# Eight unused numbers per partition behind the small tiles of a two-layer diffusion step in float32

## The chip, the cores and the metric

The kernel runs on one core of one Trainium2 chip. The metric is the time of one execution on the device in microseconds (us), the median of several runs; lower is better. Profiles come from one execution recorded by the hardware profiler.

## What is computed

The reference is one inference step of a backbone with two layers, all in float32. Each layer is run for 128 context tokens and for 512 latent tokens, model width 1024:

```python
h = x * (1 + sc_a) + sh_a
qa, ka, va, ub, vb, qc, kc, vc, gcf, gcb, pd = project(h, w_in)
...
mix = jnp.concatenate([y_a, y_b, y_c, y_d], axis=-1) @ w_out
x = layer_norm(alpha * x + g_a * mix, ln_w[0], ln_b[0])
h = x * (1 + sc_f) + sh_f
x = layer_norm(alpha * x + g_f * conv_ffn(h, ffn_up, ffn_conv_w, ffn_conv_b, ffn_down), ln_w[1], ln_b[1])
```

`y_a` to `y_d` are four mixers (windowed attention, spatial gating, retention in two directions, pooling); `conv_ffn` multiplies by `ffn_up` (1024 x 5632), applies a convolution of width 3 over the tokens, gates, and multiplies by `ffn_down` (2816 x 1024). `sh`, `sc` and `g` come from `silu(c) @ w_ada`.

## The kernel before

**Tiling.** The 640 tokens (128 context, 512 latent) are columns of one activation tile: `y8` holds 8 blocks of 128 features x 640 tokens. To keep float32 accuracy with TensorE's `float32r` operands, every operand is split into a high part and a rest: `hh` and `hl` for activations, `wh` and `wl` for weights. Every product is three matmuls: `wh` with `hh`, `wl` with `hh`, `wh` with `hl`.

**Weights.** A weight stage is fetched by the SP queue into a staging tile `st` (2048 numbers per partition, two buffers; `Cols`, `Vals` and `Rows`, DMA at L162 and in `Rows.dma`). `split` (L267 to L277) makes a pair `wh`, `wl` of 1024 numbers each: ScalarE copies `st` to `wh` (L275), VectorE subtracts (L276). The pairs live in a pool of 12 buffers, which also takes `wa`, the weights of the modulation (`AdaPair`), and some of `wf`, its first columns. `Stream` hands out the pairs in a fixed order and fetches the next stage when buffers come free.

**Products.** `fm` (L601 to L603, with the first ones at L1399 to L1402): weights are the stationary operand, activations move, 384 columns for the first part of the tokens (`GA`) and 256 for the rest (`GB`). `tm` (L883 to L885): activations are stationary, weights move, 256 columns. `wo` (L1497 to L1499, `w_out`) and `dn` (L1588 to L1590, `ffn_down`): activations are stationary, weights move, 512 columns. `sc` (L822, L823) are attention scores: queries `qs` stationary, keys `kh`, `kl` moving. `hT` (L570) transposes a tile `xr` by a matmul with the identity. `ada` (L216, L263) are the modulation products.

**Memory.** There are six pools in on-chip memory, one behind the other in this order: `one` (small tiles, and `hh`, `hl`, `y8`), `par` (parameters), `stg` (the two `st`), `wp` (the twelve weight buffers), `up` (25 unit tiles of 664 numbers, for everything else that is large) and `sm` (small numbers). Every tile takes a whole multiple of 32 bytes per partition. In `one` the tiles are, in bytes: `ident` 512, `bd` 512, `epsb` 32, `mhalf` 32, `hh`, `hl`, `y8` 20480 each, `cs` 64, `lgb` 64, `lgp` 32, `s0` 2048, `row` 2048, `scT` 1024, two folds of 32, `sb0` 128, `bf` 64. `ident` begins at byte 16512, a multiple of 64; so do `hh`, `hl` and `y8` (17600, 38080, 58560). The pool ends at 84576, 32 bytes past a multiple of 64. `par` is a multiple of 64 long, so `st` (88800 and 96992) and all twelve weight buffers (105184 and every 4096 after it) begin 32 bytes past a multiple of 64. A unit tile is 2656 bytes, 41.5 times 64, so unit tiles begin alternately on a multiple of 64 and 32 bytes past one. Addresses are those of the program; the trace has none.

**Order.** The program's order is written out by hand on every engine; no planner moves an instruction.

Of the kernel before, what the change touches and what calls it, by code (L numbers as in the profile page):

```python
# [8 lines left out]
F32 = mybir.dt.float32  # L9
# [5 lines left out]
P = 128  # L15
# [15 lines left out]
NT = 5  # L31
SPLIT_COL = 384
UW = 664

C_ID, C_BD, C_MASK, C_RELF, C_TRIF, C_RELB, C_TRIB = 0, 128, 256, 896, 1024, 1152, 1280
C_IQ, C_KC, C_COS, C_SIN, C_PF = 1408, 1664, 1666, 2178, 2690
# [53 lines left out]
def kernel(  # L90
# [6 lines left out]
    V, S, G, T = nc.vector, nc.scalar, nc.gpsimd, nc.tensor  # L97
# [3 lines left out]
    one = ctx.enter_context(tc.tile_pool(name="one", bufs=1))  # L101
# [10 lines left out]
    def nm(p):  # L112
        cnt[0] += 1
        return f"{p}{cnt[0]}"

    def unit(shape, name="u"):
        u = up.tile([P, UW], F32, tag="u", name=nm(name))[:, 0:math.prod(shape[1:])]
        if len(shape) == 3:
            u = u.rearrange("p (a b) -> p a b", b=shape[2])
        elif len(shape) == 4:  # L120
            u = u.rearrange("p (a b c) -> p a b c", b=shape[2], c=shape[3])
        return u
# [21 lines left out]
    folds = [one.tile([P, 4], F32, name="fold4"), one.tile([P, 2], F32, name="fold2")]  # L144
    sb0 = one.tile([P, 2, KD, 2], F32, name="sb0")
    bf = one.tile([P, 2, KD], F32, name="bf")
    hhf = hh.bitcast(F32)

    V.memset(scT, 0.0)
    V.memset(epsb, EPS)  # L150
    V.memset(mhalf, -0.5)


# [1534 lines left out]
```

## Time and profile before

| | |
|---|---|
| median of 3 runs | 1563.03 us (1561.6 to 1563.06) |
| the profiled execution, its own time | 1563.34 us |
| span of the profiled execution | 1561.6 us |
| TensorE busy with matmuls | 1529.7 us, 98% of the span |
| VectorE busy | 959.5 us, 61% |
| ScalarE busy | 609.9 us, 39% |
| GpSimd busy | 379.7 us, 24% |
| moved by DMA | 193.22 MB, 124 GB/s on average |

The span reaches from the first to the last instruction of the profile; the execution's own time has 1.7 us around it. Busy times of TensorE are modelled at their ends, so how fast it goes is better read from the distance between the starts of consecutive matmuls.

### The profile page before, as it was taken

Reading aid. Unit: us, or ns where it says so; the run is one execution under the profiler, and the core shown is the slowest. Engines: PE = TensorE matmul, PEld = TensorE weight load, DVE = VectorE, ACT = ScalarE, POOL = GpSimd, SP = SyncE. Lnnn points to the kernel's source line nnn. Section 1 sums busy time; section 2 is a strip of 40 time slices with the busy share of each in tenths; the row PEclk is TensorE's granted clock in tenths of the full one; section 3 lists DMA queues with packets and bytes.
Section 4 is the critical chain, followed back from the end, with each engine's and each line's share of the span. In section 5 each row is a group of like instructions: output and inputs, shape, how many; then the busy total and the mean of one; then the engine's idle time right before and its main releaser. Section 6 shows DMA issues by size and latency. Waiting matters only on the chain.

```text
span 1561.6 us, 24577 instructions
## 1 busy us (share of the span) xinstructions
PE 1529.7 (98%) x9734; PEld 1358.4 (87%) x9734; DVE 959.5 (61%) x1891; ACT 609.9 (39%) x993; POOL 379.7 (24%) x458
## 2 busy tenths in 40 slices
PE   8999999999999999999999999899999999999997
PEld 5988878899999999988789988688999999998885
DVE  4775346786556655745577665567866666674456
ACT  2544462344333333533346443524433333343331
POOL 0302266054101101200013033823531101020104
PEclk9999999999999999999999999999999999999999
DMA  9644415245343443333216355161332221224311
GB/s 326 211 152 129 136 55 202 73 130 189 120 151 116 155 137 134 109 117 124 72 38 220 123 163 175 62 202 55 126 104 82 81 81 56 81 93 130 132 38 67
DMA packets 123343, 193.22 MB, mean 124 GB/s; under 512 B 11884, under 2 KB 80566, under 8 KB 123229
## 3 DMA queue, kind: packets, MB, share of 16 engines
q1 hardware_dynamic: 114701, 166.64, 32.1%
q0 software_dynamic: 8528, 25.03, 5.0%
q8 instruction: 76, 1.25, 0.3%
q14 instruction: 38, 0.31, 0.1%
HBM read 177.97 MB, written 13.66 MB: 123 GB/s over the span
## 4 chain that ended last, share of the span: by engine, by line
PE 86%; DVE 4%; POOL 4%; ACT 2%; DMA 2%; issue 1%; SPq 0%; POOLq 0%; ACTq 0%; DVEq 0%
PE fm L601 17%; PE fm L603 16%; PE fm L602 16%; PE dn L1590 6%; PE dn L1588 6%; PE dn L1589 6%; PE ada L263 2%; PE wo L1497 2%; PE wo L1498 2%; PE wo L1499 2%; POOL on L1071 1%; DVE wl L276 1%; PE po L873 1%; PE PT L858 1%; DMA st<-in_w_in_dram 1%
## 5 line engine op out<-in xcount | busy, mean ns | idle before, releaser
L601 PE MATMUL fm<-hh,wh 128*128 128x256 f32 (+1 forms) x1888 | 589.8, 312 | 0.0
L603 PE MATMUL fm<-hl,wh 128*128 128x256 f32 (+1 forms) x1888 | 583.1, 309 | 0.9 <-DVE hl L586 0.9
L602 PE MATMUL fm<-hh,wl 128*128 128x256 f32 (+1 forms) x1888 | 582.9, 309 | 0.0
L276 DVE TENSOR_TENSOR wl<-st,wh 128x1024 fp32r<-128x1024 f32 x188 | 282.7, 1512 | 164.9 <-ACT wh L275 161.8
L601 PEld LDWEIGHTS fm<-hh,wh 128*128 128x128 f32 x1888 | 356.7, 189 | 28.1 <-ACT cv L1328 11.7
L603 PEld LDWEIGHTS fm<-hl,wh 128*128 128x128 f32 x1888 | 356.6, 189 | 1.8 <-DVE hl L586 1.1
L602 PEld LDWEIGHTS fm<-hh,wl 128*128 128x128 f32 x1888 | 356.8, 189 | 0.1
L275 ACT ACTIVATE wh<-st 128x1024 fp32r<-128x1024 f32 x188 | 196.1, 1053 | 207.2 <-PE dn L1589 141.8
L1318 DVE SCALAR_TENSOR_TENSOR cv<-fm,cwT,cv 128x127 f32<-128x127 f32 x352 | 122.0, 408 | 108.3 <-ACT cv L1315 108.2
L1590 PE MATMUL dn<-wh,hl 128*128 128x512 f32 x440 | 174.0, 395 | 0.3 <-DVE hl L1524 0.2
L1588 PE MATMUL dn<-wh,hh 128*128 128x512 f32 x440 | 174.1, 396 | 0.0
L1589 PE MATMUL dn<-wl,hh 128*128 128x512 f32 x440 | 173.8, 395 | 0.0
L1315 ACT ACTIVATE cv<-fm,cwT 128x384 f32<-128x384 f32 x88 | 58.8, 673 | 203.3 <-PE fm L603 187.8
L1537 POOL TENSOR_TENSOR act<-cv,cv 128x640 f32<-128x640 f32 x28 | 45.9, 1641 | 300.3 <-DVE cv L1333 247.3
L1328 ACT ACTIVATE cv<-fm,cwT 128x255 f32<-128x255 f32 x88 | 49.6, 563 | 175.8 <-PE fm L603 175.8
L1590 PEld LDWEIGHTS dn<-wh,hl 128*128 128x128 f32 x440 | 82.5, 187 | 21.4 <-DVE hl L1524 1.2
L1589 PEld LDWEIGHTS dn<-wl,hh 128*128 128x128 f32 x440 | 82.5, 187 | 20.0
L1588 PEld LDWEIGHTS dn<-wh,hh 128*128 128x128 f32 x440 | 82.5, 187 | 19.6
L1329 DVE SCALAR_TENSOR_TENSOR cv<-fm,cwT,bnd 128x1 f32<-128x1 f32 x88 | 19.1, 217 | 89.0 <-ACT cv L1328 88.9
L1537 POOL TENSOR_TENSOR y<-cv,cv 128x640 f32<-128x640 f32 x16 | 26.8, 1678 | 182.3 <-DVE cv L1333 162.6
L1497 PE MATMUL wo<-wh,hh 128*128 128x512 f32 x160 | 64.1, 401 | 0.0
L1498 PE MATMUL wo<-wl,hh 128*128 128x512 f32 x160 | 63.2, 395 | 0.0
(306 smaller groups left out, 2036.1 us busy)
## 6 DMA issues: line engine op xcount, KB each, us to landing
st<-in_ffn_up_dram SPq DMA_DIRECT2D x44, 1024.0 KB
wa<-in_w_ada_dram SPq DMA_DIRECT2D x80, 512.0 KB
st<-in_ffn_down_dram SPq DMA_DIRECT2D x88, 256.0 KB
st<-in_w_in_dram SPq DMA_DIRECT2D x20, 1024.0 KB
xr<-xd POOLq DMA_DIRECT2D x30, 256.0 KB, 8.1
wf<-in_w_first_dram SPq DMA_DIRECT2D x24, 256.0 KB
st<-in_w_out_dram SPq DMA_DIRECT2D x24, 256.0 KB
xd<-xr SPq DMA_DIRECT2D x20, 256.0 KB
```

The costliest lines, as they stand in the source:

```text
L275: S.activation(out=oh, in_=view, func=AF.Copy)
L276: eng.tensor_tensor(out=ol, in0=view, in1=of, op=ALU.subtract)
L601: T.matmul(ps, wh[:, k, :], hh[:, k, lo:hi], start=(k == 0), stop=False)
L602: T.matmul(ps, wl[:, k, :], hh[:, k, lo:hi], start=False, stop=False)
L603: T.matmul(ps, wh[:, k, :], hl[:, k, lo:hi], start=False, stop=(k == KD - 1))
L1318: V.scalar_tensor_tensor(out=o[:, a + d:b - 1 + d], in0=ps[:, a + 1 - d:b - d], scalar=cwT[:, tap, f:f + 1], in1=o[:, a + d:b - 1 + d], op ...
L1497: T.matmul(ps, hh[:, k, c0:c0 + P], wh[:, k % 2, :], start=(k == 0), stop=False)
L1498: T.matmul(ps, hh[:, k, c0:c0 + P], wl[:, k % 2, :], start=False, stop=False)
L1537: G.tensor_tensor(out=dst, in0=a, in1=g, op=ALU.mult)
L1588: T.matmul(ps, hh[:, s_, c0:c0 + P], wh[:, k % 2, :], start=(k == 0), stop=False)
L1589: T.matmul(ps, hh[:, s_, c0:c0 + P], wl[:, k % 2, :], start=False, stop=False)
L1590: T.matmul(ps, hl[:, s_, c0:c0 + P], wh[:, k % 2, :], start=False, stop=(k == KF - 1))
```

## The change

One tile of 8 numbers per partition (32 bytes) is added behind the last tile of the pool `one`, and VectorE fills it with zeros once. Nothing reads it. All pools behind `one` move up by 32 bytes: `st` to 88832, the weight buffers to 105216. `hh`, `hl`, `y8` and the other tiles of `one` stay.

```diff
+PAD2 = 8
...
     bf = one.tile([P, 2, KD], F32, name="bf")
+    pad2 = one.tile([P, PAD2], F32, name="pad2")
     hhf = hh.bitcast(F32)
 
     V.memset(scT, 0.0)
     V.memset(epsb, EPS)
+    for x in (pad2,):
+        V.memset(x, 0.0)
     V.memset(mhalf, -0.5)
```

## Rows read from the trace of the kernel before

**Rows 1.** The page: busy time of the engines, and the chain that ended last.
```profile
PE 1529.7 (98%) x9734; PEld 1358.4 (87%) x9734; DVE 959.5 (61%) x1891; ACT 609.9 (39%) x993; POOL 379.7 (24%) x458
...
PE 86%; DVE 4%; POOL 4%; ACT 2%; DMA 2%; issue 1%; SPq 0%; POOLq 0%; ACTq 0%; DVEq 0%
PE fm L601 17%; PE fm L603 16%; PE fm L602 16%; PE dn L1590 6%; PE dn L1588 6%; PE dn L1589 6%; PE ada L263 2%; PE wo L1497 2%; PE wo L1498 2%; PE wo L1499 2%; POOL on L1071 1%; DVE wl L276 1%; PE po L873 1%; PE PT L858 1%; DMA st<-in_w_in_dram 1%
```
**Rows 2.** Instructions grouped by line and shape: xcount | busy us, mean ns | idle before.
```profile
L601 PE MATMUL fm<-hh,wh 128*128 128x384 f32 x928 | 316.6, 341 | 0.0
L601 PE MATMUL fm<-hh,wh 128*128 128x256 f32 x960 | 273.2, 285 | 0.0
L1588 PE MATMUL dn<-wh,hh 128*128 128x512 f32 x440 | 174.1, 396 | 0.0
L1497 PE MATMUL wo<-wh,hh 128*128 128x512 f32 x160 | 64.1, 401 | 0.0
L883 PE MATMUL tm<-wh,hh 128*128 128x256 f32 x160 | 46.4, 290 | 0.0
L1399 PE MATMUL fm<-hh,wh 128*128 128x384 f32 x32 | 11.4, 358 | 0.2 <-ACT wh L275 0.2
```
**Rows 3.** Timeline of TensorE, fm: start us, duration us, engine and line.
```profile
508.94 0.34 PE L603 MATMUL fm<-hl,wh 128*128 128x384 f32 x1
...
512.59 0.34 PE L603 MATMUL fm<-hl,wh 128*128 128x384 f32 x1
512.76 0.28 PE L601 MATMUL fm<-hh,wh 128*128 128x256 f32 x1
...
515.48 0.28 PE L603 MATMUL fm<-hl,wh 128*128 128x256 f32 x1
```
**Rows 4.** Timeline of TensorE, dn and tm.
```profile
800.67 0.40 PE L1588 MATMUL dn<-wh,hh 128*128 128x512 f32 x1
...
803.47 0.40 PE L1588 MATMUL dn<-wh,hh 128*128 128x512 f32 x1
...
871.43 0.28 PE L884 MATMUL tm<-wl,hh 128*128 128x256 f32 x1
...
873.99 0.28 PE L885 MATMUL tm<-wh,hl 128*128 128x256 f32 x1
```
**Rows 5.** Timeline of TensorE, attention scores of three query blocks.
```profile
88.03 0.28 PE L823 MATMUL sc<-kl,qs 128*128 128x256 f32 x1
88.15 0.22 PE L822 MATMUL sc<-ckh,qs 128*128 128x128 f32 x1
...
92.17 0.39 PE L822 MATMUL sc<-kh,qs 128*128 128x384 f32 x1
92.40 0.34 PE L823 MATMUL sc<-kl,qs 128*128 128x384 f32 x1
...
96.78 0.39 PE L822 MATMUL sc<-kh,qs 128*128 128x384 f32 x1
97.01 0.34 PE L823 MATMUL sc<-kl,qs 128*128 128x384 f32 x1
```
**Rows 6.** Single lines: count, duration ns min/median/max, first and last start.
```profile
L570 PEld LDWEIGHTS hT<-ident,xr x120: 137/141/144, 295.8 to 1100.0; 128*128 128x128 f32 x120
...
L1333 DVE SCALAR_TENSOR_TENSOR cv<-fm,cwT,cv x88: 482/484/485, 344.6 to 1401.2; 128x256 f32<-128x256 f32 x88
...
L276 DVE TENSOR_TENSOR wl<-st,wh x188: 1206/1225/2640, 20.6 to 1510.4; 128x1024 fp32r<-128x1024 f32 x188
...
L1309 DVE TENSOR_TENSOR hl<-y,hh x10: 1206/1208/1224, 249.6 to 1044.8; 128x1024 fp32r<-128x1024 f32 x10
...
L275 ACT ACTIVATE wh<-st x188: 1039/1052/1077, 19.5 to 1509.3; 128x1024 fp32r<-128x1024 f32 x188
...
L1308 ACT ACTIVATE hh<-y x10: 1042/1044/1059, 248.5 to 1030.1; 128x1024 fp32r<-128x1024 f32 x10
```
**Rows 7.** Line L276 in 420 to 640 us and in 700 to 800 us.
```profile
L276 DVE TENSOR_TENSOR wl<-st,wh 128x1024 fp32r<-128x1024 f32 x30 | 53.7, 1789 | 10.0 <-ACT wh L275 10.0
...
L276 DVE TENSOR_TENSOR wl<-st,wh 128x1024 fp32r<-128x1024 f32 x12 | 14.7, 1224 | 37.9 <-ACT wh L275 37.9
```
**Rows 8.** The two stretches, all engines: us, busy (x count), PEclk, DMA share, GB/s.
```profile
420.00:640.00 220.00, 220.00 (x1511) 206.01 (x1510) 129.69 (x269) 73.89 (x103) 24.54 (x19) 1.00 0.39 133
700.00:800.00 100.00, 100.00 (x440) 80.37 (x439) 53.43 (x77) 33.71 (x46) 5.30 (x11) 1.00 0.27 87
```
**Rows 9.** Timeline of the start: VectorE, then TensorE's weight loads, [idle before <- releaser].
```profile
1.07 0.06 DVE L150 MEMSET epsb<- 128x1 f32 x1
1.08 0.06 DVE L151 MEMSET mhalf<- 128x4 f32 x1
4.11 0.16 DVE L1423 TENSOR_TENSOR fold<-ident 128x4 f32<-128x4 f32 x1 [2.97 <-DMA ident<-in_consts_dram]
...
8.95 0.18 PEld L216 LDWEIGHTS ada<-wf,scT 128*32 128x32 f32 x2 [0.48 <-DMA wf<-in_w_first_dram]
9.63 0.18 PEld L216 LDWEIGHTS ada<-wf,scT 128*32 128x32 f32 x2 [0.51 <-DMA wf<-in_w_first_dram]
10.30 0.14 PEld L216 LDWEIGHTS ada<-wf,scT 128*32 128x32 f32 x2 [0.48 <-DMA wf<-in_w_first_dram]
10.96 0.14 PEld L216 LDWEIGHTS ada<-wf,scT 128*32 128x32 f32 x2 [0.52 <-DMA wf<-in_w_first_dram]
11.64 0.14 PEld L216 LDWEIGHTS ada<-wf,scT 128*32 128x32 f32 x2 [0.55 <-DMA wf<-in_w_first_dram]
```
**Rows 10.** The longest pieces of the chain: start us, us, what.
```profile
8.26 11.21 DMA st<-in_w_in_dram
...
208.35 4.61 DMA st<-in_w_out_dram
```

## The prediction

> **What bounds the kernel.** I read the page first. TensorE is busy for 98% of the span, and of the chain that ended last 86% is TensorE; VectorE, the busiest of the others, has 4% of the chain [rows 1]. So only two things can move the time much: the pace at which matmuls follow each other, or a wait for staged weights that now ends earlier or later. I therefore went to the groups by line and shape for the counts and to the timeline for the pace.
>
> The counts [rows 2] stand for one of three equal lines each: fm has 3 x (928 + 32) = 2880 matmuls of 384 columns and 3 x 960 = 2880 of 256; dn and wo have 3 x (440 + 160) = 1800 of 512; tm has 3 x 160 = 480 of 256. The pace is the distance from start to start. In fm, 21 steps from 508.94 to 512.59 us make 173.8 ns for 384 columns, and 23 steps from 512.76 to 515.48 us make 118.3 ns for 256 [rows 3]. In dn, 12 steps from 800.67 to 803.47 us make 233.3 ns for 512, and in tm 22 steps from 871.43 to 873.99 us make 116.4 ns for 256 [rows 4]. Together this is 2880 x 173.8 + 2880 x 118.3 + 1800 x 233.3 + 480 x 116.4 ns = 1317 us, 84% of the span. These are the instructions whose weight operand moves.
>
> **The change, part by part.**
>
> *The new memset.* VectorE gets one more memset of 128x8. The nearest are 128x1 and 128x4, 0.06 us each, and after them VectorE is idle for 2.97 us until a DMA lands [rows 9]. That wait covers it: 0. Without the cover it would cost 0.06 us.
>
> *Staging on VectorE and ScalarE.* The splits L275 and L276 read and write tiles that begin 32 bytes past a multiple of 64. The same work on tiles that begin on a multiple of 64 already stands in the trace: L1308 and L1309 go from `y8` to `hh` and `hl`. VectorE takes 1206/1225 ns (shortest/median) for the first and 1206/1208 for the second, ScalarE 1039/1052 against 1042/1044 [rows 6]. L1333 writes `cv`, a unit tile, of which half begin on a multiple of 64 and half off it: all 88 lie between 482 and 485 ns [rows 6]. The offset costs these engines 17 ns at most (1225 - 1208), on engines that are not the bound; 188 x 17 ns = 3.2 us of VectorE's time, and on the chain L276 has 1%, 15.6 us, of which 17/1225 is 0.2 us. I take 0, with 0.2 us as the lower end. That L276 is long on average is another matter: in a stretch where GpSimd is busy 11% it means 1789 ns, where GpSimd is busy 5%, 1224 [rows 7, 8].
>
> *Unit tiles and small tiles.* All move by 32 bytes, so those that began on a multiple of 64 leave it and the others reach it. There are 25, and L1333 shows no difference between the two kinds: 0.
>
> *DMA into the moved tiles.* The first `wf` tiles are unit tiles, and consecutive ones begin alternately on a multiple of 64 and off it. The matmuls that wait for them start at 8.95, 9.63, 10.30, 10.96 and 11.64 us: 0.68, 0.67, 0.66 and 0.68 us apart, no alternation [rows 9]. So a transfer of 256 KB does not land sooner on either: 0. The rule that would say otherwise is in the Trainium skill, DMA: Bandwidth & Descriptors, section How a descriptor splits into AXI transactions: reads start at a 256-byte boundary and bytes before the start are fetched in vain. The staging tiles go from 224 to 0 bytes past such a boundary; if it held for the destination, a packet of 1024 bytes would need 32 beats in place of 39, an estimate from the page, and an 18% shorter staging transfer would take at most 2.8 us off the two pieces of 11.21 and 4.61 us in which the chain follows one [rows 10]; the sum would be near 1560. The `wf` tile that begins on a 256-byte boundary is the one that lands at 11.64 us, and its 0.68 us is no shorter than the rest.
>
> *Matmuls.* This is the only term that could decide. `hh` and `hl` stay on a multiple of 64; the weights reach it. No row shows the weights there, so I bound it. Per column, the paces are 0.4526 ns (fm 384), 0.4621 (fm 256), 0.4557 (dn) and 0.4547 (tm). In fm the off-64 operand is stationary, in dn, wo and tm it moves, and the four lie within 2%: which operand is off hardly shows. For the gain, let all come down to the best: fm 256 by 2.4 ns to 115.9, dn and wo by 1.6 ns to 231.7, tm by 0.5 ns: 2880 x 2.4 + 1800 x 1.6 + 480 x 0.5 ns = 10.0 us. For the loss, let fm 384 go to dn's pace, 175.0 ns, and tm to that of fm 256: 2880 x 1.2 + 480 x 1.9 ns = 4.4 us. The nearest row is a score matmul of 256 columns whose `kl` and `qs` both begin on a multiple of 64: its successor starts 0.12 us later, fm's 118.3 again [rows 5]. With `qs` off 64, the `kh` of 384 columns that is on 64 is followed after 0.23 us (92.17 to 92.40) and the one that is off it after 0.23 us too (96.78 to 97.01) [rows 5]. As the stationary operand, `xr` in L570 begins on a multiple of 64 in some loads and off it in others, and 120 loads lie within 137 to 144 ns [rows 6]. I take 0, with ends of -10.0 and +4.4 us.
>
> *Sum.* 0. Against the profiled execution's own 1563.34 us that is 1563.34; the median of the runs lies 0.3 us below it, so I forecast 1563.0. About 0.2%, 3.1 us, is what a measurement of this kernel can tell from no change; the three runs span 1.5 us.
>
> **The rivals.**
>
> *Weight loads or moving weights get cheaper (faster, 0.10).* For it: fm 256 takes 1.9 ns more than tm 256, and the difference between them is which operand is off 64. If that is the cause, 2880 x 1.9 = 5.5 us go and the time is 1557.5; with all of the bound it is 1553. Against it: the score row with both operands on 64 shows no such gain [rows 5].
>
> *One operand off 64 holds back every product (faster, 0.02).* Each of the 8040 products has exactly one operand off 64 now and none after. The clock granted is full, 2.4 GHz [rows 8], at which 384, 256 and 512 columns at one per cycle are 160.0, 106.7 and 213.3 ns. If the excess came from the offset, 2880 x 13.8 + 2880 x 11.6 + 1800 x 20.0 + 480 x 9.7 ns = 114 us would go: 1449. The same score row speaks against it. The Trainium skill, TensorE: Matmul & The Clock Gate, section Back-to-back issue gap, gives N/2.4 + 2.5 ns; by that rule 8040 x 2.5 ns less would go, and the time would be 1469, an estimate from the page. The trace disagrees with that rule by some 17 ns at 512 columns.
>
> *The long splits were long because of the offset (faster, 0.03).* With 1225 ns in place of the mean the chain's 15.6 us for L276 would shrink by about a fifth, 3.1 us: 1559.9. Against it, rows 7 and 8: they are long where GpSimd works.
>
> *Both operands on the same step of 64 bytes get in each other's way (slower, 0.10).* The place is fm 384, where the moving rows are on 64 already and the loads for the next matmul would now be read in step with them. The price is the upper end, 4.4 us: 1567.4. It decides from 1.1 ns per matmul (3.1 us / 2880). For it: nothing but that two operands on 64 is new for every product. Against it: the score row again.
>
> *That the layout doesn't move* would give 1563.0 as well, and lies in the forecast.
>
> **How the numbers follow.** No change has 0.75: every operand kind has a row on both sides of 64, and none differs. Faster is 0.10 + 0.02 + 0.03 = 0.15, slower 0.10. Within 0.2% of the forecast is 1559.9 to 1566.1, which holds 0.75; the staging rival ends at its edge. Down to 1557.5 about half of the first rival comes in, so 1557.5 to 1566.1 holds a little over 0.8.
>
> **What would show it.** Right: the steps of fm stay at 173.8 and 118.3 ns, dn's at 233.3, tm's at 116.4; L276 keeps 1206 as its shortest and L275 its 1052; the new memset stands near 1.1 us with VectorE idle behind it. Wrong: a step of fm 256 at 116 ns (first rival), steps near 160, 107 and 213 (second), a mean of L276 near 1225 (third), a step of fm 384 at 175 or more (fourth). A time that moves with all these unchanged would refute the view that only pace and staging count.

## The result, and the profile after

The changed kernel takes 1542.74 us (median of 4 runs, 1540.83 to 1544.91) where the kernel before takes 1562.78 in the same job: a ratio of 0.9875, 95% interval 0.986 to 0.989. The forecast was 1563.0 and no change. The profiled execution took 1542.5 us, its span is 1540.7 us, 20.9 us shorter.

The page of the changed kernel, busy times first and then two of its costliest groups (xcount | busy us, mean ns of one | idle before), answers to [rows 1] and [rows 7]; four lines were added, so L276 is now L280:

```profile
PE 1508.5 (98%) x9734; PEld 1346.0 (87%) x9734; DVE 957.4 (62%) x1892; ACT 609.7 (40%) x993; POOL 380.3 (25%) x458
...
L280 DVE TENSOR_TENSOR wl<-st,wh 128x1024 fp32r<-128x1024 f32 x188 | 282.0, 1508 | 162.1 <-ACT wh L279 159.0
...
L279 ACT ACTIVATE wh<-st 128x1024 fp32r<-128x1024 f32 x188 | 196.0, 1053 | 200.9 <-PE dn L1593 138.0
```

TensorE has lost 21.2 us of busy time with matmuls, VectorE, ScalarE and GpSimd have kept theirs within 2.1 us, and TensorE is again busy for 98% of the span. The granted clock is not what changed: it is 1.00 from 330 to 660 us in both kernels, and 0.994 before and 0.993 after over the whole execution. So the matmuls themselves follow each other faster at the same clock. The timeline of TensorE in the changed kernel shows which (start us, duration us, engine and line); it answers to [rows 3, 4]:

```profile
473.01 0.34 PE L606 MATMUL fm<-hh,wl 128*128 128x384 f32 x1
...
476.83 0.34 PE L607 MATMUL fm<-hl,wh 128*128 128x384 f32 x1
477.00 0.28 PE L605 MATMUL fm<-hh,wh 128*128 128x256 f32 x1
...
479.61 0.28 PE L607 MATMUL fm<-hl,wh 128*128 128x256 f32 x1
...
748.72 0.39 PE L1593 MATMUL dn<-wl,hh 128*128 128x512 f32 x1
...
781.23 0.40 PE L1594 MATMUL dn<-wh,hl 128*128 128x512 f32 x1
```

From 473.01 to 476.83 us are 22 steps of fm with 384 columns: 173.6 ns, as before. From 477.00 to 479.61 are 23 steps with 256 columns: 113.5 ns in place of 118.3. From 748.72 to 781.23 are 142 steps of dn: 228.9 ns in place of 233.3. Averaged over all stretches of at least 13 equal matmuls without a gap, the steps are, in ns, before and after: fm 384 173.6 and 173.7, fm 256 118.3 and 113.8, dn 233.3 and 228.9, wo 233.3 and 229.0, tm 117.0 and 117.3. With the counts of [rows 2], 2880 x 4.4 + 1800 x 4.4 ns = 20.6 us are gone and 2880 x 0.1 + 480 x 0.3 ns = 0.4 us came back: 20.2 us of the 20.9. (These means are good to some 0.2 ns.) Added up directly, from the start of each matmul to the next start on TensorE, fm 256 takes 13.1 us less, dn and wo together 7.1 us less and fm 384 0.6 us more; the rest of the difference lies outside these products.

The start of the changed kernel, VectorE's timeline, has the new memset where it was expected, with idle time behind it:

```profile
1.08 0.07 DVE L154 MEMSET pad<- 128x8 f32 x1
1.10 0.06 DVE L155 MEMSET mhalf<- 128x4 f32 x1
4.04 0.17 DVE L1427 TENSOR_TENSOR fold<-ident 128x4 f32<-128x4 f32 x1 [2.89 <-DMA ident<-in_consts_dram]
```

### The profile page after: what moved, and what is told of

It reads as the page before. It is cut to its first block, busy times and chain, and to the rows that moved or that the text cites. A ratio compares the mean times of both kernels' runs of the same rounds, so it can differ in the third digit from the quotient of the medians.

```text
span 1540.7 us, 24578 instructions
## 1 busy us (share of the span) xinstructions
PE 1508.5 (98%) x9734; PEld 1346.0 (87%) x9734; DVE 957.4 (62%) x1892; ACT 609.7 (40%) x993; POOL 380.3 (25%) x458
## 4 chain that ended last, share of the span: by engine, by line
PE 79%; DVE 4%; POOL 4%; ACT 2%; issue 1%; POOLq 0%; ACTq 0%; DVEq 0%
PE fm L605 16%; PE fm L607 15%; PE fm L606 15%; PE dn L1594 6%; PE dn L1592 6%; PE dn L1593 6%; PE ada L267 2%; PE wo L1501 2%; PE wo L1503 2%; PE wo L1502 2%; POOL on L1075 1%; DVE wl L280 1%; PE PT L862 1%; ACT h L585 1%; POOL p L1116 1%
## 5 line engine op out<-in xcount | busy, mean ns | idle before, releaser
L280 DVE TENSOR_TENSOR wl<-st,wh 128x1024 fp32r<-128x1024 f32 x188 | 282.0, 1508 | 162.1 <-ACT wh L279 159.0
L279 ACT ACTIVATE wh<-st 128x1024 fp32r<-128x1024 f32 x188 | 196.0, 1053 | 200.9 <-PE dn L1593 138.0
L1594 PE MATMUL dn<-wh,hl 128*128 128x512 f32 x440 | 173.3, 394 | 0.5 <-DVE hl L1528 0.5
L1503 PE MATMUL wo<-wh,hl 128*128 128x512 f32 x160 | 63.0, 394 | 0.0
```

The source lines that it names most:

```text
L279: S.activation(out=oh, in_=view, func=AF.Copy)
L280: eng.tensor_tensor(out=ol, in0=view, in1=of, op=ALU.subtract)
L1503: T.matmul(ps, hl[:, k, c0:c0 + P], wh[:, k % 2, :], start=False, stop=(k == KD - 1))
L1594: T.matmul(ps, hl[:, s_, c0:c0 + P], wh[:, k % 2, :], start=False, stop=(k == KF - 1))
```

## The experiments

In what follows the *distance* is the start of a weight tile minus the start of `hh`, modulo 256 bytes. `hl` and `hh` are a multiple of 256 apart, as are the twelve buffers, and so are the offsets of all blocks within a tile, so one number describes every product of a kernel. The kernel before has 32, the changed one 64. The three questions of the first four runs were: is it the weights, is it their place modulo 64, or is it the distance?

**The weights alone.** In place of the new tile in `one`, one pool of 32 bytes stands ahead of the weight buffers and one behind them, so that staging, unit and small tiles keep their place modulo 64.

```diff
+    padw_pool = ctx.enter_context(tc.tile_pool(name="padw", bufs=1))
     wp = ctx.enter_context(tc.tile_pool(name="wp", bufs=NW))
+    padu_pool = ctx.enter_context(tc.tile_pool(name="padu", bufs=1))
     up = ctx.enter_context(tc.tile_pool(name="up", bufs=NU))
...
+    padw = padw_pool.tile([P, 8], F32, name="padw")
+    padu = padu_pool.tile([P, 8], F32, name="padu")
...
```

> Only the twelve weight buffers move by 32 bytes, onto a multiple of 64; the staging tiles stay 32 bytes off, unit tiles and small tiles keep their place modulo 64. Theory A (the pace of matmuls depends on where the weights begin): the whole gain, about 1543 us, with steps of fm 256 at 113 ns and of dn at 229 ns. Rival (staging, DMA or unit tiles carry the gain): near 1563 us, steps unchanged at 118 and 233 ns.

1547.35 us (1542.2 to 1550.54), a ratio of 0.9889 (0.9866 to 0.9913). The weights carry the gain: dn stands at 228.9 ns, and staging and unit tiles have not changed their place modulo 64; of the DMA targets only `wa` and the `wf` tiles that lie in the weight buffers have. The lowest of the four runs, 1542.2 us, reaches the changed kernel. The profiled one is the slowest, 1550.54 us, and its timeline shows something new, fm with 256 columns in the first layer and in the second:

```profile
477.41 0.28 PE L607 MATMUL fm<-hh,wh 128*128 128x256 f32 x1
...
480.02 0.28 PE L609 MATMUL fm<-hl,wh 128*128 128x256 f32 x1
...
1201.99 0.28 PE L607 MATMUL fm<-hh,wh 128*128 128x256 f32 x1
...
1204.70 0.28 PE L609 MATMUL fm<-hl,wh 128*128 128x256 f32 x1
```

23 steps make 113.5 ns in the first and 117.8 ns in the second. At this distance fm has two paces. From 1100 to 1383 us, in the second layer's `ffn_up`, every stretch of 256 columns went at the second and every one of 384 columns at 176.7 ns in place of 173.2; in the first layer's, until 640 us, nearly all went at the first. In the profile of the changed kernel both layers' `ffn_up` went at the first, but for a few stretches at its beginning and end; fm in the projections ahead of it took now one pace and now the other. Added up from start to start, fm takes 6.9 us more in this profile than in that of the changed kernel, of the 8.0 us between their spans.

**Everything by 64 bytes.** `PAD2 = 16`: the weights are off 64 again, distance 96.

> Sixteen unused numbers in place of eight: all pools behind move by 64 bytes, the weights are again 32 bytes past a multiple of 64. Theory A1 (the weights' place modulo 64 decides): back to about 1563 us, steps 118 ns (fm 256) and 233 ns (dn). Rival A2 (the distance that counts is longer than 64 bytes, or any other place than the old one will do): a time that is neither 1563 nor need be 1543, and steps that differ from 118 and 233 ns.

1562.03 us, ratio 0.9998 (0.9987 to 1.0008). A memset of the same kind, all pools moved, and no gain: the place decides, not that something was moved or added. The timeline of this run has 23 steps of 118.7 ns in fm:

```profile
472.17 0.28 PE L604 MATMUL fm<-hh,wh 128*128 128x256 f32 x1
...
474.90 0.28 PE L606 MATMUL fm<-hl,wh 128*128 128x256 f32 x1
```

**The activations moved as well, and both off 64.** In the third run the eight numbers stand ahead of `hh` and not behind the small tiles: weights on a multiple of 64, `hh` 32 past one, distance 32 as before. In the fourth they stand in both places: both operands 32 past a multiple of 64, distance 64.

```diff
+    pada = one.tile([P, 8], F32, name="pada")
     hh = one.tile([P, KD, W], F32R, name="hh")
...
```

> Eight unused numbers ahead of hh in place of behind the small tiles: weights on a multiple of 64 as in the changed kernel, but hh, hl and y8 32 bytes past one, so that the distance from activations to weights is as in the kernel before. Theory R (the distance between the two operands decides): about 1563 us, steps 118 and 233 ns. Theory A1 (the weights' own place decides): about 1543 us, steps 113 and 229 ns. If both operands need a multiple of 64: in between or slower, with fm 384, whose moving operand now is off, above 173.6 ns.

> Eight unused numbers ahead of hh and eight behind the small tiles: activations and weights both begin 32 bytes past a multiple of 64, their distance is that of the changed kernel. Theory R (distance): about 1543 us, steps 113 ns (fm 256) and 229 ns (dn). Theory A1 (own place): 1563 us or slower, with no step of fm 256 under 118 ns.

The third took 1561.13 us, ratio 0.9989 (0.9978 to 0.9999); the fourth 1544.45 us, ratio 0.9882 (0.9862 to 0.9901). So a multiple of 64 is neither enough nor needed: with the weights on one and the old distance the gain is gone, and with both operands off it and the new distance it is there. The timelines of TensorE agree. The third run, fm 256 and dn:

```profile
472.68 0.28 PE L604 MATMUL fm<-hh,wh 128*128 128x256 f32 x1
...
475.39 0.28 PE L606 MATMUL fm<-hl,wh 128*128 128x256 f32 x1
...
757.11 0.39 PE L1592 MATMUL dn<-wl,hh 128*128 128x512 f32 x1
...
790.24 0.39 PE L1593 MATMUL dn<-wh,hl 128*128 128x512 f32 x1
```

That is 117.8 ns (23 steps) and 233.3 ns (142 steps), the paces of before. The fourth run, the same two:

```profile
469.95 0.28 PE L605 MATMUL fm<-hh,wh 128*128 128x256 f32 x1
...
472.56 0.28 PE L607 MATMUL fm<-hl,wh 128*128 128x256 f32 x1
...
749.74 0.39 PE L1593 MATMUL dn<-wl,hh 128*128 128x512 f32 x1
...
782.25 0.39 PE L1594 MATMUL dn<-wh,hl 128*128 128x512 f32 x1
```

113.5 ns and 228.9 ns, the paces of after.

**Other distances.** Four more values of `PAD2`, 24, 40, 56 and 48, give distances 128, 192, 0 and 224.

> All pools behind the small tiles move by 96 bytes: weights on a multiple of 64, their distance from hh 128 past a multiple of 256 (32 before, 64 in the changed kernel). Theory R64 (any distance that is a multiple of 64 will do): about 1543 us, steps near 113 ns (fm 256) and 229 ns (dn). Rival R128 (the place within 128 or 256 bytes counts too): steps that differ from both kernels by more than 1 ns, time elsewhere than 1543 by more than 4 us.

> All pools behind the small tiles move by 160 bytes: weights on a multiple of 64, distance from hh 192 past a multiple of 256. Theory R64: about 1543 us, steps near 113 and 229 ns. Rival R128: if only the place within 128 bytes counts, the same as the changed kernel (distance 64 past a multiple of 128), and the run of 96 bytes differs; if 256 counts, neither.

> All pools behind the small tiles move by 224 bytes: weights on a multiple of 64, distance from hh a multiple of 256. Theory R64: about 1543 us, steps near 113 and 229 ns. Rival (both operands on the same place of 256 bytes get in each other's way): slower than 1543, with steps of fm 384 above 175 ns. If 128 bytes count, the same as the run of 96 bytes.

> All pools behind the small tiles move by 192 bytes: weights 32 bytes past a multiple of 64, distance from hh 224 past a multiple of 256. Theory R64: about 1562 us, steps near 118 and 233 ns, as in the kernel before and in the run of 64 bytes. Rival: another place within 256 bytes is better or worse than the kernel before by more than 4 us although it is off 64.

1566.85, 1558.55, 1555.41 and 1564.17 us (ratios 1.0032, 0.9977, 0.9952 and 1.0005; intervals 1.0021 to 1.0043, 0.9966 to 0.9988, 0.9933 to 0.9972, 0.9993 to 1.0016). The theory that any distance that is a multiple of 64 will do has fallen: 128 is slower than before, 192 and 0 win a little, 64 wins most. Each kind of product has its own best place. The mean steps, worked out as above, in ns:

| distance | run | fm 384 | fm 256 | tm 256 | dn 512 | median us |
|---|---|---|---|---|---|---|
| 32 | before | 173.6 | 118.3 | 117.0 | 233.3 | 1562.8 |
| 32 | activations too | 173.6 | 118.3 | 117.0 | 233.3 | 1561.1 |
| 64 | changed | 173.7 | 113.8 | 117.3 | 228.9 | 1542.7 |
| 64 | both off 64 | 173.7 | 114.3 | 117.3 | 228.9 | 1544.5 |
| 64 | weights alone | 174.8 | 115.6 | 117.5 | 229.0 | 1547.4 |
| 96 | all by 64 | 173.7 | 118.6 | 119.9 | 233.4 | 1562.0 |
| 128 | all by 96 | 176.0 | 118.6 | 119.0 | 233.0 | 1566.9 |
| 192 | all by 160 | 173.3 | 117.7 | 114.6 | 233.3 | 1558.6 |
| 224 | all by 192 | 175.1 | 117.5 | 118.2 | 233.3 | 1564.2 |
| 0 | all by 224 | 173.6 | 119.6 | 119.6 | 226.9 | 1555.4 |

fm 256 and tm 256 are mirror images: in fm the weights are stationary and `hh` moves, in tm it is the other way, and what fm does at 64 tm does at 192 (113.8 and 114.6), at 0 both take 119.6, at 128 118.6 and 119.0. So for these products what counts is the start of the stationary operand minus that of the moving one. One stretch of tm at 192:

```profile
858.98 0.28 PE L887 MATMUL tm<-wl,hh 128*128 128x256 f32 x1
...
861.49 0.28 PE L888 MATMUL tm<-wh,hl 128*128 128x256 f32 x1
```

22 steps make 114.1 ns. Some of these means are mixtures of two paces. At 192 as at 64, products of 256 columns go at about 113.5 to 114.4 or at about 117.8 ns: tm goes at the faster in 2 of its 18 stretches at 64 and in 16 at 192, fm in most at 64 and in 3 of 107 at 192. So the distance and its sign set which pace is usual, not which one is possible. At 224 the 175.1 ns of fm 384 are stretches near 173.3 and near 176.7. At distance 0, dn is faster still than in the changed kernel, while fm 256 is slower than before; the timeline of that run:

```profile
473.52 0.28 PE L604 MATMUL fm<-hh,wh 128*128 128x256 f32 x1
...
476.27 0.28 PE L606 MATMUL fm<-hl,wh 128*128 128x256 f32 x1
...
755.86 0.40 PE L1592 MATMUL dn<-wl,hh 128*128 128x512 f32 x1
...
788.08 0.39 PE L1593 MATMUL dn<-wh,hl 128*128 128x512 f32 x1
```

23 steps of 119.6 ns and 142 of 226.9 ns.

**All distances in one run, and one distance for each product.** The weight buffers are made 256 bytes longer, so that a pair can begin at any of these places. They are now 17 x 256 bytes apart in place of 16 x 256, so that the same place in two neighbouring buffers differs by an odd multiple of 256 bytes. The first kernel walks through all distances in steps of 16 bytes; the second takes 64 for fm, 0 for dn and wo, and 192 for tm. `off`, in numbers of 4 bytes, is `4 * (k % 16)` in the first, with `k` counting the pairs of a kind, and in the second 8 for `Cols`, 56 for `Rows` and 40 for `Vals`.

```diff
+    def wtile(shape, dt, name, off=0):
+        t = wp.tile([P, D + 64], dt, tag="w", name=nm(name))[:, off:off + D]
+        return t.rearrange("p (a b) -> p a b", b=shape[1]) if len(shape) == 2 else t
...
+        wh = wtile(shape, F32R, "wh", off)
+        wl = wtile(shape, F32R, "wl", off)
```

> Each weight buffer is made 256 bytes longer, and the k-th pair of its kind (columns, values, rows) begins 16 x (k mod 16) bytes into its buffers, so that one run passes through all distances from hh in steps of 16 bytes modulo 256, counted from 32. Theory R256 (the pace of a matmul depends on the distance of its two operands modulo 256): the steps at the distances tried so far come back, for fm 256 about 113 ns at 64, 118 at 32, 96 and 128, 119.5 at 0; for dn about 227 ns at 0, 229 at 64, 233 at the others; the time lies between 1545 and 1565 us. Rival (the place of a whole pool, of staging or of unit tiles carries it): the same step at every distance, 118 and 233 ns, and about 1562 us.

> The longer buffers again, with one offset for each kind of product: distance weights minus hh 64 modulo 256 for fm, 0 for dn and wo, 192 for tm. Theory R256: fm 256 at 113 to 115 ns, dn and wo at 227 ns, tm at 115 ns; against the changed kernel another 1800 x 2.1 ns for dn and wo and 480 x 2.7 ns for tm, 5.1 us, so about 1538 us. Rival (512 bytes or more count, or one offset for all is needed): 1543 us or more, with a step of dn of 229 ns or more.

The walk took 1563.75 us in its one run. In fm 256 the gain is a single narrow place: 118.5 ns at 48, 114.0 at 64, 118.7 at 80 (some 175 steps each); no other distance is under 116.8. One stretch of each of the three, in this order:

```profile
458.28 0.28 PE L612 MATMUL fm<-hh,wh 128*128 128x256 f32 x1
...
460.99 0.28 PE L614 MATMUL fm<-hl,wh 128*128 128x256 f32 x1
...
467.26 0.28 PE L612 MATMUL fm<-hh,wh 128*128 128x256 f32 x1
...
469.88 0.28 PE L614 MATMUL fm<-hl,wh 128*128 128x256 f32 x1
...
474.26 0.28 PE L612 MATMUL fm<-hh,wh 128*128 128x256 f32 x1
...
476.99 0.28 PE L614 MATMUL fm<-hl,wh 128*128 128x256 f32 x1
```

23 steps make 117.8, 113.9 and 118.7 ns. In dn it lies at 240 and 0, 227.6 and 227.9 ns, with 231.7 at 16. One value did not come back: dn at 64 took 233.3 ns here (60 steps) and 228.9 in the changed kernel. Each pair has few matmuls here, its neighbours lie at other distances, and the buffers are spaced otherwise; which of these matters is not shown.

The second kernel took 1541.08 us (1538.93 to 1549.04), ratio 0.9881 (0.9852 to 0.991): 114.0 ns for fm 256, 115.2 for tm, 226.8 for dn. The paces came as expected; the time was 1.7 us less than the changed kernel's, not 5, with a spread of 10 us. With buffers 17 x 256 bytes apart fm at 64 and dn at 0 keep the paces that they had with 16 x 256, so for these places multiples of 256 bytes make no difference.

**Side by side.** Both were measured once more, beside each other on one chip, in five and four runs.

> The changed kernel itself, unaltered, beside the next one on the same chip. About 1543 us. At this distance fm has two paces, 272 and 416 cycles of 2.4 GHz or 283 and 424, and a stretch of matmuls without a gap keeps the one it began with: if that is chance, single runs spread from 1541 to about 1551 us, as in the run in which the weights alone moved; if the layout decides it, they stay within 4 us.

> The kernel with an offset for each kind of product (64 for fm, 0 for dn and wo, 192 for tm), unaltered. Theory R256: its median lies 3 to 5 us under that of the changed kernel in the same job, about 1539 us, since dn and wo keep 227 ns in every run. Rival (the two paces of fm outweigh it): medians within 2 us of each other.

The changed kernel took 1542.57 us (1542.0 to 1551.72), ratio 0.9887 (0.9867 to 0.9908); the other 1540.38 us (1539.59 to 1542.15), ratio 0.9865 (0.985 to 0.988). One run of the changed kernel came near 1552: the expectation had that spread for the case that the two paces are chance, and it fits; this run has no trace of its own. The timeline of the second kernel has fm at 113.5 ns and dn at 226.8 (23 and 142 steps):

```profile
476.52 0.28 PE L612 MATMUL fm<-hh,wh 128*128 128x256 f32 x1
...
479.13 0.28 PE L614 MATMUL fm<-hl,wh 128*128 128x256 f32 x1
...
747.32 0.40 PE L1600 MATMUL dn<-wl,hh 128*128 128x512 f32 x1
...
779.53 0.39 PE L1601 MATMUL dn<-wh,hl 128*128 128x512 f32 x1
```

Against the changed kernel's trace 3.2 us are gone from dn and wo, added up from start to start; wo, at 227.4 ns, has gained less than dn. The medians differ by 2.2 us, between what the theory and its rival expected, and their intervals overlap: that it beats the changed kernel is likely, and not settled.

## Why the prediction was wrong

**The step that failed is the term for matmuls.** I took 0, with ends of -10.0 and +4.4 us; it was -20.2 us: 2880 x 4.4 ns from fm 256 and 1800 x 4.4 ns from dn and wo, less 0.4 us. Two parts of the working led there.

*The row taken for nearest did not stand for the change.* The score matmul of [rows 5] has both operands on a multiple of 64, and I read it as the case after the change. But by the program's addresses this `qs`, the stationary operand, begins at byte 167616 and this `kl` at 162304; the difference is 192 modulo 256, and at 192 fm 256 takes 117.7 ns in the table above, just the 118 of the score row. The row was right and answered another question. The loads of L570, also read as a sign that the place doesn't matter, show how long one load takes and not the pace of pairs of load and matmul. The comparison of fm with tm and dn failed for the same reason: it varied which operand is off 64, at distances of 32 and, with the roles exchanged, 224, and both are slow places.

*The bound was no bound.* "Let all come down to the best" took the best pace per column of the trace, 0.4526 ns, as a floor. After the change fm 256 has 0.4445 ns (113.8/256) and dn 0.4471 (228.9/512). All four paces of the kernel before were held up by some 8 to 11% over one column per cycle at 2.4 GHz, and a price that is in every row can't be seen by comparing rows. The second rival named that excess, and for all four kinds; some of it is gone in two of them. What remains over one cycle per column is 16 cycles in fm 256 (113.5 ns, its fast pace, is 272 cycles) and 37 in dn (228.9 ns is 549).

**The rival of cheaper weight reads** had the right sign and the place of the larger part, at a chance of 0.10. Its mechanism, a multiple of 64, is refuted by the third and fourth runs, and its price of 5.5 us was too small: that its sign came out right is luck. The rival of long splits is out: L280 still means 1508 ns. The slower rival, two operands on the same step of 64, does not hold for the changed kernel, but its kind exists: at distance 128 fm 384 takes 176.0 ns and the kernel is 0.3% slower than before.

**What held.** The memset costs nothing: 0.07 us ahead of 2.89 us of idle time. Staging is as indifferent as [rows 6] said; lines L279 and L280 of the page mean 1053 and 1508 ns after 1053 and 1512 before. So are the moved staging tiles as DMA targets, and the unit tiles: the run of the weights alone has the gain in its lowest run with their places modulo 64 unchanged, and the run of 64 bytes moves them all without any. The rule on 256-byte boundaries of the Trainium skill (DMA: Bandwidth & Descriptors, How a descriptor splits into AXI transactions) is about reads; taken for the destination, as in the prediction's estimate from the page, it would have given up to 2.8 us from the moved staging tiles. The traces speak against it: packets of 1024 bytes, nearly all of which go to `st`, have a median of 46 ns in all fourteen traces, and a mean of 49.3 to 49.7 ns in the three with `st` on a 256-byte boundary and of 50.1 to 51.1 in the others, some 1 to 3% and not 18. The rule of the second rival in the Trainium skill, TensorE: Matmul & The Clock Gate, section Back-to-back issue gap, N/2.4 + 2.5 ns, is called there the gap of an isolated matmul, with another figure for a stream of loads and matmuls, so the prediction took it further than the section does. No kernel here comes to it: at 512 columns the best is 226.8 ns where the formula gives 215.8, an estimate from the page.

**What stays open.** That the pace depends on the distance of the two operands, and not on the place of either by itself, is shown by the third and fourth runs; that it is the distance modulo 256 is shown for fm at 64 and dn at 0, and not for dn at 64, which lost its gain in the walk. Why the distance counts is not shown: that the load of the next weights and the reading of the moving rows get in each other's way would be one reason, and no run tests it. Nor is it known what sets the pace with which a stretch begins.

## What to carry to other kernels

Where TensorE is the bound, read the distance between the starts of equal matmuls, divide by the columns and compare with one column per cycle: an excess that every row shares is not a floor. Eight unused numbers in the right place are a cheap trial, and the place to vary is the distance between the stationary and the moving operand in steps of 32 bytes or less through 256, for each shape of product by itself. An argument that takes a row of the trace for the case after a change of layout has to match everything the change sets, here the distance and its sign, not only the property the change is named for.

## What the runs showed of the hardware that was not expected

- In float32r products the pace depends on the start of the stationary operand minus that of the moving one, modulo 256 bytes: by that difference 256 columns take from 113.8 to 119.9 ns, and the good place for fm 256 is narrower than 16 bytes on either side. With 512 columns, where only weights moved, the pace goes from 226.9 to 233.4 ns.
- At a distance of 64, fm has two paces, 113.5 and 117.8 ns for 256 columns, 173.2 and 176.7 for 384. An unbroken sequence kept one for 270 us; that made most of the 8.0 us by which the profiled run of the weights alone was longer than that of the changed kernel.
- VectorE, ScalarE and DMA showed next to no difference between tiles on a multiple of 64 bytes and 32 past one: the splits' medians are 1226 and 1051 ns after and 1225 and 1052 before, and packets of 1024 bytes have a median of 46 ns in both.
